# Seventeen unread transposes of the identity at the start, and two tiles' second halves put one place later, in an encoder layer's kernel

## The chip, the cores and the metric

One core of a Trainium2 chip runs the whole program; the other cores are idle. The metric is the device time of one execution in microseconds (us), and less is better. TensorE (PE) does the matrix products, VectorE (DVE) and ScalarE (ACT) the elementwise work, GpSimd (POOL) and SyncE (SP) mostly issue DMAs.

## What is computed

One encoder layer on 1024 tokens of width 1024, in float32: a half-step feed-forward block, two groups of attention heads side by side, and a second half-step feed-forward block. The change touches only the first microseconds of the first block:

```python
def rmsnorm(x, g):
    xf = x.astype(jnp.float32)
    y = xf * lax.rsqrt(jnp.mean(xf * xf, axis=-1, keepdims=True) + NORM_EPS)
    return (y * g.astype(jnp.float32)).astype(x.dtype)

def swiglu(x, w_gate, w_up, w_down):
    return (jax.nn.silu(x @ w_gate) * (x @ w_up)) @ w_down
...
        h = swiglu(rmsnorm(x, ffn1_pre_g[l]), ffn1_w_gate[l], ffn1_w_up[l], ffn1_w_down[l])
        x = x + 0.5 * rmsnorm(h, ffn1_post_g[l])
...
```

## The kernel before, in words

**Tiles.** The 1024 tokens are eight tiles of 128 rows. A tile `t` is loaded, normalised (`xn`), and turned on TensorE in two halves of 512 columns: four transposes of 128x128 fill one PSUM bank (`trp`, pool `pst`, two banks). ScalarE rounds the bank to a high part, VectorE subtracts to get the low part. The first halves of tiles 0 to 3 make up operand `A11` (`x_161` high, `x_162` low), the second halves `A12` (`x_163`, `x_164`). `Operand.one(t)` turns the next half of tile `t`; with a list `later` it puts off the copy and the store (`keep`) of that half.

**Products.** Every product is three TensorE passes, high by high (L354), high by low (L355), low by high (L356), and is called for four slices of 128 rows (`ks`), so one block of 512 columns is 12 matmuls. The gate weights come in column blocks b = 0, 1, 2, ...: `graw` is loaded by SP (L480), ACT casts it to `whi` (L453), DVE subtracts to `wlo` (L454), in `split_left`. Blocks 0 to 2 are handled by hand in `begin`; from block 3 on `PairGemm.ahead` does them. In its order TensorE computes block 0 with A12, block 1 with A12, block 3 with A11, block 2 with A12, block 4 with A11, block 3 with A12, and so on. After a block's A12 product VectorE adds the kept A11 result (L657, tile `s`, in place) and ScalarE applies SiLU (L659), whose first use loads a table. The A11 result was copied from PSUM by `save` (L472) and stored to memory (`s1d<-s`).

**Order.** Inside `begin` a manual schedule fixes the order of TensorE, VectorE and ScalarE as the code is written. `begin` ends by giving VectorE and ScalarE back to the scheduler; only TensorE stays in written order. From there on the scheduler places the casts, subtractions, SiLUs and squares of `ahead`, by its own estimate of when each is ready. `c.step()` runs inside `PairGemm.mm` after every second slice: it takes one step off the list `c.steps`, so that a half-tile's transposes can be put in the middle of a product.

**Start.** The gain row is spread over 128 partitions by two float32 matmuls with one row of ones (L341, `gps`). Before them TensorE has nothing to do, and after them it waits for the first normalised tile. Then it turns the first halves of tiles 0 and 1, multiplies blocks 0 and 1 by their 256 columns, turns the first halves of tiles 2 and 3, and finishes. In the last loop of `begin`, over the three blocks, the second halves of tiles 0 to 3 are turned.

Of the kernel before, what the change touches and what calls it, by code (L numbers as in the profile page):

```python
# [10 lines left out]
F32 = mybir.dt.float32  # L11
# [8 lines left out]
P, T = 128, 512  # L20
# [148 lines left out]
def transposed(c, x, bank=False):  # L169

    ps = (c.psm.tile([P, 4, P], F32, tag="mm", name="trp") if bank else
          c.pst.tile([P, 4, P], F32, tag="tr", name="trp"))
    for j in range(4):
        c.nc.tensor.transpose(ps[:, j, :], x[:, j * P:(j + 1) * P], c.ident)  # L174
    return ps


def transpose_in(c, x, hi, lo):

    ps = transposed(c, x)  # L180
    c.nc.scalar.copy(hi, ps)
    c.nc.vector.tensor_sub(lo, ps, hi.bitcast(F32))  # L182
    return ps


class Operand:
# [59 lines left out]
    def one(self, t, later=None):  # L246
# [6 lines left out]
        if t < 4:  # L253
            if t not in self.raw:
                two = c.xp.tile([P, 2, 2, 4, P], F32, tag="s", name="raw", bufs=c.deep)
                self.raw[t], self.raw[t + 1] = two[:, 0], two[:, 1]
            raw, i = self.raw[t], 0 if b == A11 else 1
            hi, lo = [h[:, :, cols] for h in self.x[b]]

            def keep():  # L260
                c.nc.scalar.copy(raw[:, i], ps)
                c.nc.gpsimd.dma_start(self.saved[t][:, i], raw[:, i].rearrange("p k x -> p (k x)"))
            if later is None:
                ps = transposed(c, src)
                c.nc.scalar.copy(hi, ps)
                keep()
                c.nc.vector.tensor_sub(lo, raw[:, i], hi.bitcast(F32))
            else:
                ps = transpose_in(c, src, hi, lo)
                later.append(keep)  # L270
        elif b == A11:
            while self.open == c.deep:
                c.sums.popleft()()
            self.open += 1
            self.left_half(t, src)
        else:
            self.right_half(t, src, cols)

    def left_half(self, t, src):

        c = self.c
        s = c.xp.tile([P, 4, 4, P], F32, tag="s", name="s", bufs=c.deep)
        c.nc.scalar.copy(s[:, 0], transposed(c, src, t > 4))
        self.half[t] = s, self.half[t]
# [49 lines left out]
def spread_gain(c, t, row, one):  # L334

    nc = c.nc
    copies = []
    for h in range(2):
        sl = slice(h * T, h * T + T)
        ps = c.psm.tile([P, T], F32, tag="mm", name="gps")  # L340
        nc.tensor.matmul(ps, one, row[:, sl], start=True, stop=True)  # L341
        copies.append(lambda sl=sl, ps=ps: nc.scalar.copy(t[:, sl], ps))
    return t, *copies
# [998 lines left out]
def layer(tc, a, out):  # L1342
    nc = tc.nc
    c = Ctx(tc)
    with ExitStack() as ctx:
# [81 lines left out]
        def ffn(which, op, prep, pg, get, turns, sums, more, post, pre, src, dst, begin=None, tables=()):  # L1427
# [7 lines left out]
            if begin:  # L1435
                left_pool(e)
            begun = begin(pg) if begin else ()
            plan(pg.early, turns)
            r = sub()
# [119 lines left out]
        with ExitStack() as order:  # L1559
# [16 lines left out]
            op0 = Operand(c, None, 0)  # L1576
            nc.gpsimd.memset(xn[1][:1, :P], 1.0)
            for t in range(2):
                for h, q in enumerate((nc.sync, nc.scalar)):
                    q.dma_start(xs[t][:, half[h]], x0[t][:, half[h]])  # L1580
                    if (t, h) == (0, 0):
                        nc.sync.dma_start(xn[0][:1], a["ffn1_pre_g"])
            op0.gain, *gains = spread_gain(c, gain, xn[0][:1], xn[1][:1, :P])

            def begin(pg):
                for b in range(2):
# [62 lines left out]
                keeps = []  # L1649
# [26 lines left out]
                scaled(r1, 1, 2, 3)  # L1676
                hi2(1)
                for b in range(3):
                    if b == 1:
                        c.steps.extend(lambda t=t: op0.one(t) for t in range(2))  # L1680
                    elif b:
                        op0.one(2, keeps)
                        c.steps.append(lambda: op0.one(3, keeps))
                    pg.mm(acc[b], pg.w[b], 0, A11, cols=slice(256 if b < 2 else 0, 512))
                    s1.append(pg.save(b, acc[b]))
                    (lo0, lo1, lo2)[b](1)
                while keeps:
# [8 lines left out]
                                    {0: [F(4, 5), L(6, 7)], 2: [F(6, 7)], 3: [U(4)], 5: [U(5)], 6: [U(6)], 7: [U(7)]},  # L1696
                                    down_sums(a["wd1"], ts1), value_sums(a["wv"], tsv),
                                    a["ffn1_post_g"], a["mix_pre_g"], x0, x1, begin,
                                    bias_steps(c, *[a[k] for k in ("na_rel_bias", "t5_rel_bias", "onehot", "lncount", "cmask")]))

# [293 lines left out]
```

## Time and profile before

| | us |
|---|---|
| median of 3 runs | 1843.02 (1842.95 to 1844.0) |
| the profiled execution, its own time | 1842.29 |
| its span, first to last instruction | 1840.3 |
| TensorE busy | 1817.0 (99%) |
| VectorE busy | 1329.6 (72%) |
| ScalarE busy | 829.9 (45%) |
| GpSimd busy | 322.4 (18%) |

The span is 1.99 us shorter than the execution's own time, and that execution is 0.73 us below the median of the three runs. Times in the views are counted from the first instruction. In a timeline a row gives start, duration, engine, line, operation, output and inputs, and in brackets the idle time before it with what ended it; matmuls overlap, so their pace is read from start to start. In a view by windows each row gives the stretch, then the busy time of each engine with the number of instructions, the clock granted to TensorE, the share of the DMA engines and their rate.

### The profile page before, as it was taken

How to read it: one execution, taken by the hardware profiler on the slowest of the kernel's cores; microseconds unless marked ns; L12 is line 12 of the kernel's file. 1: busy time of each engine (PE TensorE's matmuls, PEld its weight loads, DVE VectorE, ACT ScalarE, POOL GpSimd, SP SyncE). 2: the span in 40 equal slices, each digit the busy share in tenths (PEclk: the TensorE clock that was granted, in tenths of full speed). 3: DMA queues.
4: the chain of work that ended last, by engine and by line, in shares of the span. 5: the costliest groups of instructions: out<-in, count | busy, mean ns of one | idle time of the engine just before them, and what ended most of it. 6: DMA issues, size and time to landing. Idle time of an engine off the chain costs nothing.

```text
span 1840.3 us, 25143 instructions
## 1 busy us (share of the span) xinstructions
PE 1817.0 (99%) x8904; PEld 1527.5 (83%) x8904; DVE 1329.6 (72%) x2243; ACT 829.9 (45%) x1479; POOL 322.4 (18%) x508
## 2 busy tenths in 40 slices
PE   7999999999999999999999999999999999999998
PEld 6887888888888888888899998878888888888886
DVE  5878877776566877477777866778888777754557
ACT  6622233334443657133688765564222333354433
POOL 2223211111121122132333100121111111110000
PEclk9999999999999999999999999999999999999999
DMA  7756565657888857869686532595556566596564
GB/s 274 240 176 226 170 227 208 222 184 252 315 295 314 285 198 260 275 209 305 201 276 217 183 125 94 184 311 183 178 169 212 191 218 233 183 343 204 186 226 150
DMA packets 172991, 409.66 MB, mean 223 GB/s; under 512 B 20081, under 2 KB 42513, under 8 KB 170818
## 3 DMA queue, kind: packets, MB, share of 16 engines
q1 hardware_dynamic: 124706, 246.33, 40.6%
q0 software_dynamic: 47152, 159.64, 23.7%
q10 hardware_dynamic: 1008, 2.10, 0.3%
q8 instruction: 70, 1.15, 0.3%
q14 instruction: 55, 0.45, 0.1%
HBM read 280.49 MB, written 132.56 MB: 224 GB/s over the span
## 4 chain that ended last, share of the span: by engine, by line
PE 89%; DVE 4%; ACT 2%; issue 2%; DMA 2%; POOL 0%; SPq 0%; DVEq 0%; POOLq 0%; ACTq 0%
PE mmp L356 17%; PE mmp L354 17%; PE mmp L355 17%; PE accp L354 10%; PE accp L356 10%; PE accp L355 10%; PE po L1161 2%; PE po L1274 2%; PE ptp L1057 2%; PE trp L174 1%; PE sp L1258 1%; PE sp L1140 1%; DVE pw L738 1%; ACT pb L1049 1%; DMA s1d<-s 0%
## 5 line engine op out<-in xcount | busy, mean ns | idle before, releaser
L354 PE MATMUL mmp<-x,whi 128*128 128x512 f32 (+1 forms) x1464 | 572.7, 391 | 1.7 <-ACT whi L453 1.1
L356 PE MATMUL mmp<-x,wlo 128*128 128x512 f32 (+1 forms) x1464 | 570.2, 389 | 3.8 <-DVE wlo L454 3.8
L355 PE MATMUL mmp<-x,whi 128*128 128x512 f32 (+1 forms) x1464 | 570.1, 389 | 0.5 <-DVE x L182 0.3
L356 PEld LDWEIGHTS mmp<-x,wlo 128*128 128x128 f32 x1464 | 276.2, 189 | 62.2 <-DVE wlo L454 5.5
L354 PEld LDWEIGHTS mmp<-x,whi 128*128 128x128 f32 x1464 | 276.1, 189 | 59.9 <-issue 1.7
L355 PEld LDWEIGHTS mmp<-x,whi 128*128 128x128 f32 x1464 | 276.2, 189 | 56.9 <-DVE x L182 1.2
L738 DVE TENSOR_TENSOR pw<-praw,pw 128x1024 fp32r<-128x1024 f32 (+1 forms) x181 | 200.4, 1151 | 122.4 <-ACT pw L737 121.9
L737 ACT CAST pw<-praw 128x1024 fp32r<-128x1024 f32 (+1 forms) x181 | 168.4, 981 | 204.7 <-PE accp L356 167.7
L354 PE MATMUL accp<-pw 128*128 128x512 f32 x600 | 234.4, 391 | 0.0
L356 PE MATMUL accp<-pw 128*128 128x512 f32 x600 | 233.6, 389 | 0.0
L355 PE MATMUL accp<-pw 128*128 128x512 f32 x600 | 233.5, 389 | 0.0
L453 ACT CAST whi<-wraw 128x1024 fp32r<-128x1024 f32 x126 | 132.4, 1053 | 221.3 <-PE mmp L355 182.9
L454 DVE TENSOR_TENSOR wlo<-wraw,whi 128x1024 fp32r<-128x1024 f32 x126 | 154.6, 1229 | 20.5 <-ACT whi L453 19.2
L356 PEld LDWEIGHTS accp<-pw 128*128 128x128 f32 x600 | 112.6, 188 | 23.5
L355 PEld LDWEIGHTS accp<-pw 128*128 128x128 f32 x600 | 112.7, 188 | 23.2
L354 PEld LDWEIGHTS accp<-pw 128*128 128x128 f32 x600 | 112.7, 188 | 23.2 <-ACT hb L781 0.2
L453 ACT CAST whi<-traw 128x512 fp32r<-128x512 f32 x52 | 32.3, 622 | 157.6 <-DVE traw L545 104.4
L680 POOL DMA_DIRECT2D g<-sg x44 | 23.9, 543 | 428.6 <-DVE sg L673 239.9
L632 DVE TENSOR_TENSOR c<-mmp,u 128x512 f32<-128x512 f32 x52 | 35.9, 691 | 72.8 <-PE mmp L356 72.7
L472 ACT COPY s<-mmp 128x512 f32<-128x512 f32 x52 | 30.6, 588 | 121.3 <-PE mmp L356 113.9
L544 DVE TENSOR_TENSOR wraw<-wraw 128x1024 f32<-128x1024 f32 x52 | 63.6, 1223 | 13.1 <-DMA wraw<-in_wu_dram 12.2
L619 DVE TENSOR_TENSOR c<-mmp,v 128x512 f32<-128x512 f32 x52 | 35.7, 686 | 32.5 <-PE mmp L356 32.5
(286 smaller groups left out, 2775.4 us busy)
## 6 DMA issues: line engine op xcount, KB each, us to landing
praw<-g SPq DMA_DIRECT2D x70, 512.0 KB, 5.7
wraw<-in_wg_dram SPq DMA_DIRECT2D x44, 512.0 KB, 4.2
wraw<-in_wu_dram SPq DMA_DIRECT2D x44, 512.0 KB, 6.8
tr<-in_wd_dram SPq DMA_DIRECT2D x44, 512.0 KB, 6.6
g<-sg POOLq DMA_DIRECT2D x88, 256.0 KB, 5.0
ts<-tr POOLq DMA_DIRECT2D x22, 1024.0 KB, 4.7
praw<-ts SPq DMA_DIRECT2D x88, 256.0 KB, 3.8
praw<-in_wd_dram SPq DMA_DIRECT2D x66, 256.0 KB, 5.6
```

Of the source, the lines that this page charges most:

```text
L354: nc.tensor.matmul(out, ahi, bhi, start=start, stop=False, skip_group_check=go_on)
L355: nc.tensor.matmul(out, ahi, blo, start=False, stop=False, skip_group_check=go_on)
L356: nc.tensor.matmul(out, alo, bhi, start=False, stop=stop, skip_group_check=go_on)
L453: nc.scalar.copy(hi, raw)
L454: nc.vector.tensor_sub(lo, raw, hi.bitcast(F32))
L544: nc.vector.tensor_sub(r[:, 0:2], r[:, 1:3], r[:, 0:2])
L632: c.behind(lambda: nc.vector.tensor_add(c21, d, u2), *((DVE,) if self.sink.soon and b == self.n - 1 else ()))
L737: nc.scalar.copy(hi, raw[:, :m])
L738: nc.vector.tensor_sub(lo, raw[:, :m], hi.bitcast(F32))
L1057: nc.tensor.transpose(ps[:, j, :], src[:, j * P:(j + 1) * P], c.ident)
L1161: nc.tensor.matmul(po[:, un * 2 + j], pt[:, 2 * j + t, :], rhs, start=t == 0, stop=t == 1)
L1274: nc.tensor.matmul(po[0][:, u], pt[0][:, j, :], vs[:, k0 + j, :], start=j == 0, stop=j == n - 1)
```

## The change

A new helper `turned(c, n)` takes a `trp`-sized bank and turns the identity into it n times; nothing reads the bank. It is called with 13 ahead of the two gain matmuls and with 4 behind them. In the last loop of `begin` the second halves of tiles 2 and 3 are both queued as steps inside block 2's product; before, tile 2 was turned ahead of that product, and tile 3 was its first step.

```diff
+def turned(c, n):
+
+    ps = c.pst.tile([P, 4, P], F32, tag="tr", name="turned")
+    for j in range(n):
+        c.nc.tensor.transpose(ps[:, j % 4, :], c.ident, c.ident)
...
+            turned(c, 13)
             op0.gain, *gains = spread_gain(c, gain, xn[0][:1], xn[1][:1, :P])
+            turned(c, 4)
...
                 for b in range(3):
-                    if b == 1:
-                        c.steps.extend(lambda t=t: op0.one(t) for t in range(2))
-                    elif b:
-                        op0.one(2, keeps)
-                        c.steps.append(lambda: op0.one(3, keeps))
+                    if b:
+                        c.steps.extend(lambda t=t: op0.one(t, *([keeps] if t > 1 else [])) for t in (2 * b - 2, 2 * b - 1))
                     pg.mm(acc[b], pg.w[b], 0, A11, cols=slice(256 if b < 2 else 0, 512))
```

Seven lines come ahead of everything that is named here, so L354 of before is L361 of after, L453 is L460, and so on.

TensorE in block 2's product, before (`trp<-ident,x` turns a half of tile 2 or 3, `x_161` is A11, `x_163` is A12; the first row turns tile 1):

```order
L174 MATMUL trp<-ident,xn 128x128 x4
L174 MATMUL trp<-ident,x 128x128 x4
L354 MATMUL mmp<-x_161,whi 128x512
L355 MATMUL mmp<-x_162,whi 128x512
L356 MATMUL mmp<-x_161,wlo 128x512
L354 MATMUL mmp<-x_161,whi 128x512
L355 MATMUL mmp<-x_162,whi 128x512
L356 MATMUL mmp<-x_161,wlo 128x512
L174 MATMUL trp<-ident,x 128x128 x4
```

Six more matmuls of A11 follow there, then block 0's A12 product. The same engine after, from the middle of block 2's product to the first A12 matmuls:

```order
L174 MATMUL trp<-ident,x 128x128 x4
L361 MATMUL mmp<-x_161,whi 128x512
L362 MATMUL mmp<-x_162,whi 128x512
L363 MATMUL mmp<-x_161,wlo 128x512
L361 MATMUL mmp<-x_161,whi 128x512
L362 MATMUL mmp<-x_162,whi 128x512
L363 MATMUL mmp<-x_161,wlo 128x512
L174 MATMUL trp<-ident,x 128x128 x4
L361 MATMUL mmp<-x_163,whi 128x512
L362 MATMUL mmp<-x_164,whi 128x512
```

Each of the two sets of transposes has moved six matmuls later, and tile 3's now stands right in front of the product that reads it.

ScalarE behind `begin`, before (`x2` squares tiles 4 and 5; `whi<-graw` are the weight blocks 3, then 4; `s_362` and `s_399` are the results of blocks 0 and 1):

```order
L166 ACTIVATE xn,ss<-x 128x1024 x2
L659 ACT_TABLE_LOAD
L659 ACTIVATE s_362<-s_362 128x512
L453 CAST whi<-graw 128x1024
L659 ACTIVATE s_399<-s_399 128x512
L166 ACTIVATE xn,ss<-x 128x1024
L453 CAST whi<-graw 128x1024
```

And after (the same two results are `s_381` and `s_418`):

```order
L166 ACTIVATE xn,ss<-x 128x1024 x2
L460 CAST whi<-graw 128x1024
L666 ACT_TABLE_LOAD
L666 ACTIVATE s_381<-s_381 128x512
L460 CAST whi<-graw 128x1024
L666 ACTIVATE s_418<-s_418 128x512
L166 ACTIVATE xn,ss<-x 128x1024
```

The scheduler has moved the cast of block 3 ahead of the table load and the first SiLU, and the cast of block 4 ahead of the second SiLU and a square.

VectorE at the same place, before (`wlo<-graw,whi` is block 3; `s_399` is the sum for block 1; the small rows are the scale factors of tiles 4 and 5, the L226 row their normalisation):

```order
L151 TENSOR_SCALAR y<-y 128x2
L157 TENSOR_TENSOR e<-y,v 128x2
L158 TENSOR_TENSOR e<-e,y 128x2
L159 SCALAR_TENSOR_TENSOR y<-e,y 128x2
L157 TENSOR_TENSOR e<-y,v 128x2
L158 TENSOR_TENSOR e<-e,y 128x2
L159 SCALAR_TENSOR_TENSOR y<-e,y 128x2
L157 TENSOR_TENSOR e<-y,v 128x2
L158 TENSOR_TENSOR e<-e,y 128x2
L657 TENSOR_TENSOR s_399<-mmp,s_399 128x512
L159 SCALAR_TENSOR_TENSOR y<-e,y 128x2
L226 SCALAR_TENSOR_TENSOR xn<-x,y,gain 128x1024
```

The row behind these is L454, the subtraction for block 3. After, from the same row on:

```order
L151 TENSOR_SCALAR y<-y 128x2
L461 TENSOR_TENSOR wlo<-graw,whi 128x1024
L157 TENSOR_TENSOR e<-y,v 128x2
L158 TENSOR_TENSOR e<-e,y 128x2
L159 SCALAR_TENSOR_TENSOR y<-e,y 128x2
L664 TENSOR_TENSOR s_418<-mmp,s_418 128x512
```

The subtraction for block 3 has moved ahead of the sum for block 1 and of a normalisation. Apart from the places named here, the order of the instructions on each engine is the same in both programs, save that the subtraction for block 4 and the pieces of the scale factors also change places next to these rows.

## The prediction

> **What bounds the kernel now.** I read the page first, then the busy time in 40 windows.
>
> ```profile
> span 1840.3 us, 25143 instructions
> PE 1817.0 (99%) x8904; PEld 1527.5 (83%) x8904; DVE 1329.6 (72%) x2243; ACT 829.9 (45%) x1479; POOL 322.4 (18%) x508
> ```
> ```profile
> 46.00:92.00 46.00, 46.00 (x218) 38.09 (x217) 37.97 (x63) 30.02 (x49) 9.61 (x18) 1.00 0.70 240
> ```
>
> TensorE sets the time: of 1840.3 us it is idle for 23.3, and from 46 us on it is full. All that the change moves lies ahead of 46 us. Behind it every load is issued as a buffer is given back, that is, relative to the work, so I count a microsecond won or lost ahead of 46 us as one microsecond of the end.
>
> The timeline ahead of 46 us has one large hole, at block 3's product with A11:
>
> ```profile
> 34.02 0.50 PE L354 MATMUL mmp<-x,whi 128*128 128x512 f32 x1 [1.06 <-ACT whi L453]
> 34.35 0.40 PE L355 MATMUL mmp<-x,whi 128*128 128x512 f32 x1
> 37.31 0.50 PE L356 MATMUL mmp<-x,wlo 128*128 128x512 f32 x1 [2.56 <-DVE wlo L454]
> 40.85 0.63 PE L354 MATMUL mmp<-x,whi 128*128 128x512 f32 x1
> ```
>
> TensorE idles 1.06 us for block 3's `whi`, does two matmuls, idles 2.56 us for its `wlo`, and begins block 2's product with A12 only at 40.85. The rows of ScalarE and VectorE say why both parts are late:
>
> ```profile
> 30.88 0.21 ACT L166 ACTIVATION_READ_ACCUMULATOR xn<-x 128x1 f32 x1
> 31.11 1.28 ACT L659 ACT_TABLE_LOAD   x1
> 32.94 1.03 ACT L453 CAST whi<-graw 128x1024 fp32r<-128x1024 f32 x1
> ...
> 31.53 0.17 DVE L151 TENSOR_SCALAR y<-y 128x2 int32<-128x2 int32 x1
> 34.04 0.69 DVE L657 TENSOR_TENSOR s<-mmp,s 128x512 f32<-128x512 f32 x1 [0.77 <-DMA s1d<-s]
> 36.03 1.22 DVE L454 TENSOR_TENSOR wlo<-graw,whi 128x1024 fp32r<-128x1024 f32 x1
> ```
>
> The cast stands behind the table load and the first SiLU. The subtraction stands behind block 1's sum, which waits until 34.04 for a store of the tile that it overwrites, and then behind a normalisation. Neither waits for the weights: block 3 is asked for at 23.50 and takes 8.0 us, so it is there at 31.5.
>
> ```profile
> 23.50 16.44 SPq L480 DMA_DIRECT2D graw<-in_wg_dram  x4
> ...
> graw<-in_wg_dram SPq DMA_DIRECT2D x1, 512.0 KB, 8.0
> ```
>
> The hole has a second price. I cut the start into stretches of 3.41 us (columns: stretch, length, TensorE busy, then the others; the granted clock is third from the end):
>
> ```profile
> 4.27:7.68 3.41, 3.06 (x4) 1.16 (x4) 1.08 (x5) 2.50 (x6) 0.00 (x0) 1.00 0.99 364
> 7.68:11.09 3.41, 2.40 (x9) 1.57 (x8) 2.61 (x7) 2.74 (x5) 0.00 (x0) 1.00 1.02 377
> 11.09:14.51 3.42, 2.60 (x11) 2.08 (x10) 3.05 (x9) 2.46 (x8) 0.00 (x0) 1.00 0.32 129
> 14.51:17.92 3.41, 3.41 (x18) 3.41 (x17) 1.83 (x5) 2.30 (x5) 1.24 (x2) 1.00 0.11 44
> 34.98:38.40 3.42, 1.09 (x5) 0.92 (x6) 3.42 (x4) 2.50 (x4) 0.55 (x1) 1.00 1.00 375
> 38.40:41.81 3.41, 3.41 (x10) 2.65 (x9) 1.19 (x2) 0.59 (x1) 0.00 (x0) 0.50 1.03 416
> ```
>
> In 34.98 to 38.40 TensorE was busy for 1.09 us, and for the next 3.41 us its clock is 0.50; then it is full again. Half of that stretch, 1.7 us, is lost. It is part of the 40.85 above.
>
> **The change, part by part.**
>
> *The seventeen transposes* run where TensorE has nothing to do.
>
> ```profile
> 1.12 0.28 POOL masks.py:199 TENSOR_SCALAR_AFFINE_SELECT ident<-ident 128x128 f32<-128x128 f32 x1
> 4.62 3.75 PE L341 MATMUL gps<-xn 1*128 1x512 f32 x4 [4.62 <-DMA xn<-in_ffn_pre_g_dram]
> 9.38 1.94 PE L174 MATMUL trp<-ident,xn 128*128 128x128 f32 x8 [1.01 <-DVE xn L1615]
> 11.36 0.58 ACT L181 CAST x<-trp 128x512 fp32r<-128x512 f32 x1 [0.27 <-PE trp L174]
> 13.10 0.42 PE L356 MATMUL mmp<-x,wlo 128*128 128x256 f32 x1
> 13.31 0.41 PE L354 MATMUL mmp<-x,whi 128*128 128x256 f32 x1
> 15.44 1.06 ACT L261 COPY raw<-trp 128x512 f32<-128x512 f32 x2
> 16.51 1.72 PE L174 MATMUL trp<-ident,x 128*128 128x128 f32 x8
> 17.61 1.25 ACT L181 CAST x<-trp 128x512 fp32r<-128x512 f32 x2 [1.11 <-PE trp L174]
> 17.99 0.36 PE L354 MATMUL mmp<-x,whi 128*128 128x256 f32 x1
> ```
>
> The eight transposes from 16.51 to 17.99 take 0.185 us each, those at 9.38 at most 1.94 / 8 = 0.24. Thirteen are 2.4 to 3.1 us, from the finished identity at 1.40 to 3.8 or 4.5: ahead of the gain row that lands at 4.62. Four are 0.74 to 0.97 us, from 8.37 to 9.1 or 9.34: ahead of the normalised tile at 9.38. Their cost is 0, at most 0.1 us, and nobody waits for their bank.
>
> What they may win is the clock. At 13.10 a matmul of 256 columns starts every 0.21 us; later one of 512 columns starts every 0.23 (27.01 to 27.25 to 27.47, rows below). So TensorE runs at half pace to 17.9 or so, though the clock column shows 1.00 there; six stretches of 3.41 us ahead of 38.40 is 17.92, and the stretch that ends there was the first to be wholly busy, 3.41 of 3.41. Busy shares of 2.40, 2.60 and even 3.06 us (the gain matmuls, one row high) did not do. With the fillers a stretch of 3.41 us that begins at 0.85 holds 13 x 0.185 = 2.4 us, the next is 4.27 to 7.68 as before, and 7.68 to 11.09 gains 0.74 and holds 3.1. None is full if the stretches fall as in this execution. If they fall with a start between 4.62 and 5.7, one lies wholly inside the gain matmuls and the four transposes behind them, which is a third of the places that it can have, and that helps only if those one-row matmuls count. I take 0 for the clock, with 1.1 to 1.4 us as the other end: if it is full ahead of 13.10, the matmuls from there to 16.51 take half, tiles 2 and 3 are turned as soon as they are scaled, and their casts begin when ScalarE is free, at 15.44 + 1.06 = 16.50 and not at 17.61: 1.1 us, and 0.27 more from the earlier cast at 11.36.
>
> The Trainium skill, in TensorE: Matmul & The Clock Gate, Part 1, says that the gate watches a free-running window of 3413 ns and opens after one busy window; the two edges of the 0.50 stretch here agree. Its Part 4 says of transposes on TensorE that "it doesn't count as PE-busy the same way", which would make these seventeen worth nothing and give the same sum as mine. The trace speaks against that: of the full stretch 14.51 to 17.92, 1.41 us were transposes (from 16.51 on) and 2.0 us matmuls, and the stretch ahead of it, busy for 2.60 us with nearly nothing but matmuls, had not brought the full clock.
>
> *Tiles 2 and 3 later.* The rows of before:
>
> ```profile
> 23.54 0.66 PE L174 MATMUL trp<-ident,x 128*128 128x128 f32 x4
> 25.42 0.60 PE L174 MATMUL trp<-ident,x 128*128 128x128 f32 x4
> 26.05 0.59 ACT L181 CAST x<-trp 128x512 fp32r<-128x512 f32 x1 [0.44 <-PE trp L174]
> 26.67 0.69 DVE L182 TENSOR_TENSOR x<-trp,x 128x512 fp32r<-128x512 f32 x1
> 27.01 0.39 PE L356 MATMUL mmp<-x,wlo 128*128 128x512 f32 x1
> 27.25 0.39 PE L354 MATMUL mmp<-x,whi 128*128 128x512 f32 x1
> 27.47 0.45 PE L355 MATMUL mmp<-x,whi 128*128 128x512 f32 x1
> ```
>
> Tile 3's transposes at 25.42 are cast from 26.05 (0.63 later) and subtracted from 26.67 to 27.36, under six matmuls; the A12 product then needs the low part at 27.47, and it is there. After the change that cover is gone. Block 2's product starts some 0.27 us before 23.54, since it needn't wait for a free bank, so tile 3's transposes start at 23.27 + six matmuls 1.47 + transposes 0.35 + six matmuls 1.48 = 26.6; cast at 27.2, subtraction 27.8 to 28.5, and the second A12 matmul at 28.5 instead of 27.47. Cost 1.1 us. From below: with the transposes' own latency hidden, 0.6. The same moved step takes the stores of the two halves and the save of block 2's result 0.4 us later in POOL's queue and on ScalarE; nobody waits for these here.
>
> *The new order behind it.* Both casts and the subtraction of block 3 now stand ahead of what made them late. From 28.5 on there are 11 matmuls left of block 0 with A12, then 12 of block 1: at 0.23 us each, block 3's product is wanted at 28.5 + 23 x 0.23 = 33.8, and its third matmul, the first that needs `wlo`, at 34.3. ScalarE is through with the second square at 31.1, with the 0.4 us from above 31.5, and the weights are there at 31.5: cast to 32.5. VectorE has done L151 by then (31.7 plus at most 0.8 of the later sum for block 0), subtraction to 33.8. Both are ready, by 1.3 and 0.5 us. So no hole, and no half clock after it: block 3's twelve matmuls end at 33.8 + 12 x 0.23 = 36.6, where block 2 with A12 begins. Before that was 40.85. Gain 4.25 us, with the 1.1 us lost at tile 3 already in it.
>
> *Sum.* Fillers 0, tile 3 and the new order together -4.25: 1842.29 - 4.25 = 1838.0 by the profiled execution. That one lies 0.73 below the median of the three runs, so the same sum against the median is 1838.8.
>
> **The rivals.**
>
> 1. *The clock opens early as well.* For it: the transposes count, by the stretch to 17.92. Against it: no stretch was full in the phase of this execution. All behind 16.5 us, loads too, moves up by 1.1 to 1.4: 1836.6 to 1836.9.
> 2. *The hole comes back in part, from the memory.* The cast now stands first and would hold ScalarE until its weights land. In the same stretch a load of the same size took 9.5 us:
>
> ```profile
> x<-in_x_dram POOLq DMA_DIRECT2D x1, 512.0 KB, 9.5
> ...
> sgd<-s POOLq DMA_DIRECT2D x1, 256.0 KB, 6.9
> ```
>
> Then the weights are there at 33.0, the cast ends at 34.0 and the subtraction at 35.3, 1.0 us after TensorE wants it: 1839.0. With a short idle stretch that halves the clock again for up to 3.41 us, another 1.7: 1840.7.
> 3. *Slower: a new wait on ScalarE.* Block 0's SiLU is now behind the cast, at 33.8 to 34.5, and its store starts then. Block 3's save needs that store's buffer; at 6.9 us the store is through at 41.4, and ScalarE, in order, holds block 5's cast behind it: save 0.6, cast 1.03, subtraction 1.22, ready at 44.3. TensorE wants it after three products of 2.76 and two sets of transposes, at 36.6 + 9.0 = 45.6. It is hidden by 1.3 us. It decides when the store takes over 8.2 us, and makes the kernel slower than before by 0.2% when it takes 8.2 + 4.25 + 3.7 = 16.1 us, which no row comes near.
> 4. *That the change doesn't do what it says*: the fillers leave the clock as it is. That is my forecast.
>
> **How the numbers follow.** Forecast 0.50; early clock 0.27; part of the hole back 0.18; slower 0.05. The executions of before differ by 1.7 us, which I put down to where the stretches fall. The range 1836.0 to 1840.2 takes in the early clock below and most of the second rival above. A measurement of this kernel can tell about 0.2%, 3.7 us, from no change: the line is 1839.3. The forecast is under it by 1.3, and I give it 0.46 of its 0.50 there; the early clock all of its 0.27; the second rival 0.03 of 0.18. Faster 0.76, same 0.19, slower 0.05.
>
> **What would show it.** Right: block 3's first three matmuls in a row near 33.8 with no wait on `whi` or `wlo`; no stretch of clock 0.50 at 38; a new wait of about 1 us in front of the first A12 matmuls, on the cast and the subtraction of tile 3. The early clock shows in matmuls of 256 columns every 0.12 us at 13. Wrong: a wait of block 3 on its cast with the cast waiting for the load, or block 5 waiting for its cast.

## The result, and the profile after

The changed kernel takes 1838.11 us, the median of 9 runs (1836.71 to 1841.1), against 1843.01 for the kernel before (9 runs beside them, 1840.68 to 1844.82). The ratio is 0.9973, with a 95% interval of 0.9964 to 0.9982: 3.3 to 6.6 us faster. The forecast was 1838.0 in a range of 1836.0 to 1840.2. The profiled execution's own time is 1838.41.

The page of the changed kernel, and its first 46 us as one window (columns as in the prediction); the same window of before stands behind it:

```profile
span 1836.4 us, 25177 instructions
PE 1819.0 (99%) x8921; PEld 1529.0 (83%) x8921; DVE 1328.5 (72%) x2243; ACT 829.6 (45%) x1479; POOL 324.7 (18%) x508
0.00:46.00 46.00, 41.84 (x194) 33.19 (x195) 28.25 (x60) 30.95 (x56) 12.82 (x31) 1.00 0.74 276
```
```profile
0.00:46.00 46.00, 35.56 (x155) 27.63 (x156) 27.26 (x58) 29.72 (x53) 11.98 (x30) 0.96 0.74 274
```

TensorE's idle time ahead of 46 us has shrunk from 10.44 to 4.16 us. That is no measure of the gain, since 3.04 + 1.12 us of the new busy time are the transposes that nobody reads (that this sum is 4.16 as well is chance):

```profile
1.46 3.04 PE L182 MATMUL turned<-ident 128*128 128x128 f32 x13 [1.46 <-POOL ss L1643]
8.13 1.12 PE L182 MATMUL turned<-ident 128*128 128x128 f32 x4
```

The gain is read from where the work stands. The hole at block 3 is gone; TensorE's timeline after:

```profile
25.86 0.60 PE L174 MATMUL trp<-ident,x 128*128 128x128 f32 x4
27.14 0.50 PE L361 MATMUL mmp<-x,whi 128*128 128x512 f32 x1 [0.68 <-ACT x L188]
27.86 0.50 PE L362 MATMUL mmp<-x,whi 128*128 128x512 f32 x1 [0.22 <-DVE x L189]
...
33.19 0.39 PE L361 MATMUL mmp<-x,whi 128*128 128x512 f32 x1
...
33.64 0.39 PE L363 MATMUL mmp<-x,wlo 128*128 128x512 f32 x1
...
35.91 0.39 PE L361 MATMUL mmp<-x,whi 128*128 128x512 f32 x1
...
38.63 0.39 PE L361 MATMUL mmp<-x,whi 128*128 128x512 f32 x1
```

Tile 3's high and low part are waited for, as forecast; block 3's first three matmuls follow each other every 0.23 us; block 2 with A12 begins at 35.91 and not at 40.85. The engines that feed it, ScalarE and VectorE:

```profile
16.96 1.07 ACT L188 CAST x<-trp 128x512 fp32r<-128x512 f32 x2 [0.65 <-PE trp L174]
...
30.80 1.05 ACT L460 CAST whi<-graw 128x1024 fp32r<-128x1024 f32 x1 [0.17 <-DMA graw<-in_wg_dram]
...
31.88 1.23 DVE L461 TENSOR_TENSOR wlo<-graw,whi 128x1024 fp32r<-128x1024 f32 x1
```

Tiles 2 and 3 are cast from 16.96 (17.61 before). Block 3's cast runs at 30.80 where it ran at 32.94, the subtraction at 31.88 where it ran at 36.03. There is no half clock left. Before, the clock was 0.50 from 38.40 to 41.81; after, it is 1.00 there:

```profile
38.00:40.00 2.00, 2.00 (x11) 1.60 (x10) 1.46 (x2) 0.00 (x0) 0.00 (x0) 1.00 1.03 412
40.00:42.00 2.00, 2.00 (x13) 1.70 (x12) 0.00 (x0) 0.00 (x0) 0.00 (x0) 1.00 1.02 416
```

And there is a new wait, which the prediction had priced at nothing:

```profile
34.09 0.55 POOL L670 DMA_DIRECT2D sgd<-s  x1 [2.39 <-ACT s L666]
...
41.83 0.60 PE L174 MATMUL trp<-ident,xn 128*128 128x128 f32 x4
...
42.31 0.59 ACT L479 COPY s<-mmp 128x512 f32<-128x512 f32 x1 [6.01 <-DMA sgd<-s]
42.95 0.50 PE L361 MATMUL mmp<-x,whi 128*128 128x512 f32 x1 [0.52 <-ACT s L479]
```

Block 3's save takes over the buffer of block 0's SiLU. That tile's store is asked for at 34.09 and the save starts at 42.31. TensorE waits 0.52 us, because from block 3 on the A12 product goes on in the very PSUM bank that the save copies (VectorE adds a kept A11 result for blocks 0 to 2 only). In the kernel before, the same matmul follows its transposes without a wait:

```profile
44.03 0.39 PE L354 MATMUL mmp<-x,whi 128*128 128x512 f32 x1
...
47.23 0.60 PE L174 MATMUL trp<-ident,xn 128*128 128x128 f32 x4
47.58 0.48 PE L354 MATMUL mmp<-x,whi 128*128 128x512 f32 x1
```

From those transposes to that matmul it is 0.35 us before and 1.12 after, so the wait costs 0.77 us from start to start.

### The profile page after: what moved, and what is told of

It reads as the page before. It is cut to its first block, busy times and chain, and to the rows that moved or that the text cites. A ratio compares the mean times of both kernels' runs of the same rounds, so it can differ in the third digit from the quotient of the medians.

```text
span 1836.4 us, 25177 instructions
## 1 busy us (share of the span) xinstructions
PE 1819.0 (99%) x8921; PEld 1529.0 (83%) x8921; DVE 1328.5 (72%) x2243; ACT 829.6 (45%) x1479; POOL 324.7 (18%) x508
## 4 chain that ended last, share of the span: by engine, by line
PE 76%; issue 11%; DVE 5%; DMA 3%; ACT 2%; POOL 1%; DVEq 0%; POOLq 0%; SPq 0%; ACTq 0%
PE mmp L363 13%; PE mmp L361 13%; PE mmp L362 13%; PE accp L363 9%; PE accp L362 9%; PE accp L361 9%; PE po L1168 2%; PE po L1281 2%; PE ptp L1064 2%; PE sp L1265 1%; PE trp L174 1%; PE sp L1147 1%; DVE pw L745 1%; POOL g L711 1%; ACT pb L1056 1%
## 5 line engine op out<-in xcount | busy, mean ns | idle before, releaser
L361 PE MATMUL mmp<-x,whi 128*128 128x512 f32 (+1 forms) x1464 | 571.9, 391 | 1.9 <-ACT x L188 1.4
L361 PEld LDWEIGHTS mmp<-x,whi 128*128 128x128 f32 x1464 | 275.7, 188 | 59.8 <-ACT x L188 2.2
L361 PE MATMUL accp<-pw 128*128 128x512 f32 x600 | 234.3, 391 | 0.2 <-ACT hb L788 0.2
L460 ACT CAST whi<-wraw 128x1024 fp32r<-128x1024 f32 x126 | 132.6, 1054 | 221.3 <-PE mmp L362 182.8
L361 PEld LDWEIGHTS accp<-pw 128*128 128x128 f32 x600 | 112.6, 188 | 23.8 <-ACT hb L788 0.6
L460 ACT CAST whi<-traw 128x512 fp32r<-128x512 f32 x52 | 32.3, 621 | 157.4 <-DVE traw L552 110.3
```

Of the source, the lines that this page charges most:

```text
L361: nc.tensor.matmul(out, ahi, bhi, start=start, stop=False, skip_group_check=go_on)
L460: nc.scalar.copy(hi, raw)
```

## The experiments

Theory 1 was the prediction's: the whole gain is the scheduler's new order of block 3's cast and subtraction, and the transposes do nothing. Theory A was that the transposes open the clock early and this carries part of the gain. The first four kernels tell these apart; the other seven ask why an earlier start isn't worth more. All but `fill40` were timed in five rounds beside the kernel before (medians 1843.07, 1842.96 and 1842.95 in the three sets).

### The transposes alone

Against the changed kernel, the tiles go back to their place of before:

```diff
-                    if b:
-                        c.steps.extend(lambda t=t: op0.one(t, *([keeps] if t > 1 else [])) for t in (2 * b - 2, 2 * b - 1))
+                    if b == 1:
+                        c.steps.extend(lambda t=t: op0.one(t) for t in range(2))
+                    elif b:
+                        op0.one(2, keeps)
+                        c.steps.append(lambda: op0.one(3, keeps))
```

> Only the seventeen transposes are added; tiles 2 and 3 stay in the order of before, and with them the order of ScalarE and VectorE. Theory 1 (the whole gain comes from the order of the casts, which the moved tiles changed): about 1843, within 1 us of before, with the hole at block 3 from 34 to 37 us and the half clock after it still there. Theory 2 (the fillers open the clock early): matmuls of 256 columns start every 0.12 us at 13, and 1841.6 to 1842.

1843.02 us (11 runs), ratio 0.9999 (0.999 to 1.0008). The scheduler's orders on ScalarE and VectorE are those of before. TensorE's timeline, and a window behind the hole:

```profile
33.30 0.50 PE L361 MATMUL mmp<-x,whi 128*128 128x512 f32 x1 [1.08 <-ACT whi L460]
...
37.29 0.79 PE L363 MATMUL mmp<-x,wlo 128*128 128x512 f32 x1 [3.26 <-DVE wlo L461]
...
38.00:40.00 2.00, 2.00 (x6) 1.53 (x5) 1.56 (x2) 0.00 (x0) 0.00 (x0) 0.50 1.02 412
```

The hole and the half clock are both there. The seventeen transposes show no gain by themselves. The interval reaches from 1.8 us faster to 1.5 slower, so the 1.1 to 1.4 us of an early clock are not excluded by this time alone; in the profiled execution the matmuls of 256 columns kept their half pace up to 15.8.

### The moved tiles alone

Against the changed kernel, the transposes are left out:

```diff
-            turned(c, 13)
...
-            turned(c, 4)
```

> Only tiles 2 and 3 are moved, no fillers; ScalarE and VectorE have the order of the changed kernel. Theory 1: as the changed kernel, 1838.1, within 1 us. Theory 2 (the fillers carry 1.1 to 1.4 us of the gain): 1839.2 to 1839.5.

1838.47 us (11 runs), ratio 0.9977 (0.9968 to 0.9986): as much as the changed kernel gains, within the intervals. Tile 3's lost cover is there, the hole is not:

```profile
27.93 0.50 PE L361 MATMUL mmp<-x,whi 128*128 128x512 f32 x1 [0.68 <-ACT x L188]
...
36.72 0.39 PE L361 MATMUL mmp<-x,whi 128*128 128x512 f32 x1
```

### The new order without the move

The tiles stay where they were and no transposes are added; block 3's cast and subtraction are written ahead of block 0's sum and SiLU, so that the scheduler places them first. Against the kernel before:

```diff
                 self.mm(a, w, 1, A12, s1 is None)
+                if b == 0 and begun:
+                    self.split_left(3)
```

> The tiles stand as in before and there are no fillers, but block 3's cast and subtraction are written ahead of block 0's SiLU, so that ScalarE and VectorE get nearly the changed kernel's order. Theory 1 (the order of the casts is all of it, and the moved tiles cost TensorE 0.6 to 1.1 us): no hole at block 3, A12 of block 0 starts 0.6 to 1.1 us earlier than with the moved tiles. If nothing is late behind that, 1837.0 to 1837.5. If the save of block 3, which waits for the store of block 0's SiLU, decides the start of block 3's A12 product, it comes at the same time as before it, TensorE waits there about 1.7 us instead of 0.8, and the time is 1838.1. Theory 2 (the place of the transposes itself matters): 1843.

1838.69 us (8 runs), ratio 0.9974 (0.9964 to 0.9985). The move of the tiles is one way to the new order and not the only one. The tile's 1.1 us that this version saves are not seen in the time. In its profiled execution the first tile is turned at 11.52 (9.38 before), and block 3 waits for its weights:

```profile
34.13 1.05 ACT L453 CAST whi<-graw 128x1024 fp32r<-128x1024 f32 x1 [0.98 <-DMA graw<-in_wg_dram]
...
35.23 0.50 PE L354 MATMUL mmp<-x,whi 128*128 128x512 f32 x1 [0.25 <-ACT whi L453]
...
36.49 0.50 PE L356 MATMUL mmp<-x,wlo 128*128 128x512 f32 x1 [0.52 <-DVE wlo L454]
```

That is the prediction's second rival, at 0.77 us.

### Forty transposes

```diff
-            turned(c, 13)
+            turned(c, 40)
```

> The changed kernel with 40 transposes ahead of the gain matmuls instead of 13: at 0.22 us each at half clock they last 8.8 us from 1.5, so a stretch of 3.41 us of nothing but transposes fits wherever the stretches fall. Theory A (transposes open the clock): by 8.3 us the pace of the transposes doubles, the gain matmuls take 0.43 us each and not 0.86, the 256-column matmuls start every 0.12 us from the first. The start is delayed by 0 to 2 us, and the time is 1837 to 1840. Theory B (they do not count): the pace stays 0.21 us up to the first stretch full of matmuls, the first tile is turned some 4 us later, and the time is 1841 to 1843.

One run, 1839.86 us. TensorE's timeline:

```profile
1.46 7.03 PE L182 MATMUL turned<-ident 128*128 128x128 f32 x40 [1.46 <-POOL ss L1643]
8.42 1.98 PE L348 MATMUL gps<-xn 1*128 1x512 f32 x4
...
15.09 0.28 PE L361 MATMUL mmp<-x,whi 128*128 128x256 f32 x1
15.20 0.28 PE L362 MATMUL mmp<-x,whi 128*128 128x256 f32 x1
```

The gain matmuls take 1.98 us instead of 3.75, and matmuls of 256 columns start every 0.12 us instead of 0.21. Transposes do open the clock. By Part 4 of TensorE: Matmul & The Clock Gate, in the Trainium skill, they would not; this run decides against it. The price here is that the gain matmuls start at 8.42, 4.0 us later than in the changed kernel.

### The changed kernel again

> The changed kernel once more, beside the next three on the same chip: 1838 within 1 us, the wait of block 3's A12 product for its save 0 to 0.8 us.

1837.9 us (9 runs), ratio 0.9975 (0.9965 to 0.9984). Its profile began later (first tile turned at 10.59 and not 9.17), and the first A12 matmul of block 3 follows its transposes after 0.45 us, 0.10 more than before, not 0.77. So the size of the new wait differs from execution to execution.

### An earlier table load

A SiLU of one column inside `begin` loads ScalarE's table there, so that the table load no longer stands between block 3's cast and block 0's SiLU.

```diff
+                nc.scalar.activation(c.small.tile([P, 4], F32, tag="e", name="e")[:, :1], c.ident[:, :1], AF.Silu)
```

> The changed kernel with one SiLU of a single column on ScalarE at about 16.3 us, where it waits for TensorE, so that the table of SiLU is loaded there and not in front of block 0's SiLU. Theory 1 (block 3's save waits for the store of block 0's SiLU, and TensorE for the save): the SiLU, its store and the save come up to 1.28 us earlier, the 0.77 us that TensorE waits there are gone, and the time is 1837.3 to 1837.9, at worst 0.3 us are lost on the casts at 17. Theory 2 (that wait is covered again later): as the changed kernel.

1838.74 us (11 runs), ratio 0.998 (0.9971 to 0.9989): no gain. The table load now stands ahead of the casts of tiles 2 and 3, which begin at 17.97, for 16.96 in the changed kernel's profile; a part of that is the clock, which opened only near 18.5 here. Block 0's SiLU follows block 3's cast at once, at 33.04, and the save still waits for the store:

```profile
16.57 1.28 ACT L1672 ACT_TABLE_LOAD   x1
...
17.97 1.13 ACT L188 CAST x<-trp 128x512 fp32r<-128x512 f32 x2
...
32.08 1.05 ACT L460 CAST whi<-graw 128x1024 fp32r<-128x1024 f32 x1 [0.46 <-DMA graw<-in_wg_dram]
...
42.75 0.59 ACT L479 COPY s<-mmp 128x512 f32<-128x512 f32 x1 [5.58 <-DMA sgd<-s]
```

### The store in another queue

The stores of the first three SiLUs are issued by ScalarE, not by GpSimd.

```diff
-            nc.gpsimd.dma_start(d, sg)
+            (nc.scalar if s1 is not None else nc.gpsimd).dma_start(d, sg)
```

> The changed kernel, with the stores of the SiLU of blocks 0 to 2 issued by ScalarE's own DMA queue instead of GpSimd's. In the changed kernel the store of block 0's SiLU is asked for at 34.09 and block 3's save waits for it until 42.31, a wait that costs TensorE 0.77 us. Theory 1 (the store is late because it stands in GpSimd's queue behind the loads and stores of the tiles): on a queue of its own it lands by 40, the save stands right behind the last A11 matmul of block 3, the wait is gone, and the time is 1837.1 to 1837.5. Theory 2 (all transfers share one throughput, the queue is indifferent): it lands at 42 or later, the wait stays at 0.8 us or grows, and the time is 1838.0 to 1838.6.

1838.16 us (9 runs), ratio 0.9977 (0.9967 to 0.9986). The time is the one that this run's theory 2 forecast. The DMA issue of the store, what follows it, the stores by their group, and a window:

```profile
35.87 0.33 ACTq L670 DMA_DIRECT2D sgd<-s  x1
...
44.28 0.59 ACT L479 COPY s<-mmp 128x512 f32<-128x512 f32 x1 [5.42 <-PE trp L174]
...
sgd<-s ACTq DMA_DIRECT2D x2, 256.0 KB, 8.3
...
40.00:44.00 4.00, 4.00 (x23) 3.31 (x21) 1.42 (x2) 0.00 (x0) 0.00 (x0) 1.00 1.02 407
```

In a queue of its own the 256 KB take 8.3 us, no less than in GpSimd's. The DMA share is 1.02 there, which fits transfers that wait for each other whatever queue they are in; what they wait for is not shown. The releaser named for the save, a transpose, is put down to the wrong one: the four transposes at 43.67 write another bank, while 35.87 + 8.3 = 44.2, with the median of the two stores in that window, is about the store's landing. TensorE waits 0.66 us for the save.

### Three ways to an early clock

`rows128`: twenty transposes, and gain matmuls of 128 rows, 127 of them zero.

```diff
-            nc.gpsimd.memset(xn[1][:1, :P], 1.0)
+            nc.gpsimd.memset(xn[1][:, :P], 1.0)
+            nc.vector.memset(xn[0], 0.0)
...
-            turned(c, 13)
-            op0.gain, *gains = spread_gain(c, gain, xn[0][:1], xn[1][:1, :P])
+            turned(c, 20)
+            op0.gain, *gains = spread_gain(c, gain, xn[0], xn[1][:, :P])
```

> The changed kernel with 20 transposes ahead of the gain matmuls instead of 13, and with the gain matmuls 128 rows high instead of one: 127 rows of zeros below the gain row, ones under all of them, the same result. TensorE is then busy without a gap from 1.5 to about 9.3 us, as it nearly is in the changed kernel. Theory A (matmuls of one row do not count for the clock, transposes and full matmuls do): the clock opens by 8.3 us wherever the stretches fall, 256-column matmuls start every 0.12 us from the first, everything behind 16.5 moves up by 1.1 to 1.4, 1836.7 to 1837.0. Theory B (it is not the rows; the gain matmuls or the mix of both don't count): pace 0.21 up to 16 us or later, 1838.1, or up to 0.3 more if the gain row comes later.

1838.29 us (11 runs), ratio 0.9977 (0.9968 to 0.9986). The gain matmuls ran at full pace (1.96 us), but at 13.81 matmuls of 256 columns started every 0.21 us again: the clock had opened and closed. The save cost more here: block 3's first A12 matmul waited 0.85 us for it.

`best` adds to this the early table load and the early cast of block 3, on the tiles' order of before.

> All that should help together: tiles 2 and 3 as before the change, block 3's cast written ahead of block 0's SiLU, the table of SiLU loaded early, 20 transposes and gain matmuls of 128 rows. If the early clock gives 1.1 to 1.4, the covered casts of tile 3 0.6 to 1.1 and the earlier save lets them through: 1835.6 to 1836.4. If the weights of block 3, which come from memory, set its start: no better than the better of the two before it, 1836.7 to 1837.3, with a wait of block 3's cast for its load.

1840.45 us (11 runs), ratio 0.9988 (0.9979 to 0.9997): slower than the changed kernel and than either time that was expected. In its profile block 2 with A12 begins at 36.75 and then TensorE waits longest of all for the save:

```profile
43.90 0.59 ACT L479 COPY s<-mmp 128x512 f32<-128x512 f32 x1 [6.72 <-DMA sgd<-s]
44.54 0.50 PE L361 MATMUL mmp<-x,whi 128*128 128x512 f32 x1 [1.29 <-ACT s L479]
```

Another part lies in the early table load. It runs from 16.57 to 17.85, as in the version that has it alone, and the casts of tiles 2 and 3 stand behind it at 17.97. Here the clock had been open since 16.0 and the tiles were turned from 16.31, so TensorE waited 0.99 us for these casts; in `rows128`, with the casts at 17.25, it didn't wait. The two waits are what the rows show, in an execution whose own time is 1839.87; whether they make up the whole of some 2.3 us stays open.

`held` is `rows128` with 14 transposes behind the gain matmuls and ten more ahead of the first product, to keep the clock open; `held_act` adds the stores in ScalarE's queue.

```diff
-            turned(c, 4)
+            turned(c, 14)
...
+                for j in range(10):
+                    nc.tensor.transpose(acc[2][:, j % 4 * P:j % 4 * P + P], c.ident, c.ident)
```

> The changed kernel with 20 transposes of the identity ahead of the gain matmuls, those matmuls 128 rows high, 14 transposes behind them and ten more between the first tiles' transposes and the first product, so that an early opened clock has less idle time in which to close. Both theories expect matmuls of 256 columns every 0.12 us near 13. Theory 1 (a microsecond won at the start is one of the end): block 0's product with A12 begins 1.1 to 1.4 us earlier and the time is 1836.7 to 1837.1. Theory 2 (the memory paces blocks 3 to 5): what is won is waited for again in front of block 3's cast and its save, whose wait of 0.8 us grows to 1.5 to 2.2, and the time is 1837.6 to 1838.6.

> Both edits together: the clock kept open by transposes, and the SiLU stores of blocks 0 to 2 in ScalarE's queue. If the store's queue is what makes block 3's save wait, both gains stand: 1835.8 to 1836.5. If the memory's throughput paces the stage whatever the queue, the time is that of the other two within 0.6 us, 1837.6 to 1838.6.

1838.68 us (10 runs, ratio 0.9973, 0.9964 to 0.9983) and 1838.34 us (9 runs, 0.9975, 0.9965 to 0.9984). In the profiled execution of `held` the gain matmuls still ran at half pace (3.66 us) and the first tile was turned at 12.07, 2.9 us later than in the changed kernel; the clock opened as they ended, since the 14 transposes behind them took 1.69 us, as long as the same 14 in `held_act`. In that of `held_act` it was open before the first tile and stayed so. What became of it is seen in TensorE's and ScalarE's rows:

```profile
10.29 1.38 PE L174 MATMUL trp<-ident,xn 128*128 128x128 f32 x8
...
13.41 0.28 PE L361 MATMUL mmp<-x,whi 128*128 128x256 f32 x1
13.53 0.28 PE L362 MATMUL mmp<-x,whi 128*128 128x256 f32 x1
...
16.42 1.26 PE L174 MATMUL trp<-ident,x 128*128 128x128 f32 x8 [0.94 <-ACT raw L268]
...
15.79 1.06 ACT L268 COPY raw<-trp 128x512 f32<-128x512 f32 x2
17.11 1.19 ACT L188 CAST x<-trp 128x512 fp32r<-128x512 f32 x2 [0.26 <-PE trp L174]
```

TensorE is done with its matmuls at 15.48 and waits until 16.42 for a bank: the copies of tiles 0 and 1 out of the two `trp` banks run from 15.79 to 16.85 on ScalarE. Tiles 2 and 3 are cast from 17.11; in the changed kernel, at half pace, they were cast from 16.96. But the first tile was turned at 10.29 here and at 9.17 there. From it to these casts it is 6.82 us in `held_act`, and 6.6 to 6.8 in the other three profiles with the clock open at the first tile and no early table load (in `rows128` it was shut again in between), against 7.79 in the changed kernel and 8.23 (9.38 to 17.61) before. So the open clock does shorten this path, by 1.0 to 1.4 us, until the copies on ScalarE end it; the later first tile takes that back. How much of the lateness the added work causes isn't separated: the changed kernel's second profile has its first tile at 10.59.

## Why the prediction was right, point by point

**The bound.** It took a microsecond ahead of 46 us as one of the end. That can now be tested over many starts. From block 3's first A12 matmul to the end of the span:

| | block 3 with A12 | span | rest |
|---|---|---|---|
| before | 47.58 | 1840.3 | 1792.7 |
| transposes alone | 48.72 | 1841.5 | 1792.8 |
| after | 42.95 | 1836.4 | 1793.5 |
| after, again | 43.71 | 1837.4 | 1793.7 |
| tiles alone | 43.01 | 1836.3 | 1793.3 |
| earlier table load | 43.39 | 1835.8 | 1792.4 |
| `held_act` | 42.85 | 1836.3 | 1793.5 |
| store in ScalarE's queue | 44.92 | 1838.3 | 1793.4 |

The rest is 1792.4 to 1793.7 for starts that lie 5.9 us apart: one for one, to within 0.7 us either way. The five executions that aren't listed give 1792.6 to 1793.8. The changed kernel's execution gives back 0.7 of its 4.63 there, 0.5 of it by 500 us and 0.2 near 1230. That is inside the scatter, and what it consists of wasn't tried.

**The transposes: cost 0, gain 0.** Right as far as the times tell. Alone they give a ratio of 0.9999, and the tiles alone give the changed kernel's time. The first rival, the early clock, didn't come about: in the changed kernel's profile the pace changed at 16.33. Its size was sound: where the clock was open at the first tile, the path to the casts of tiles 2 and 3 was 1.4 us shorter than before, for 1.1 to 1.4 forecast. Those versions turn their first tile 1.1 to 2.9 us later than the changed kernel's first profile, so their times don't show it. The rival's step "tiles 2 and 3 are turned as soon as they are scaled" also fell short, since they need the banks that ScalarE's copies hold; that put the casts 0.26 behind the copies.

**Tile 3's lost cover: 1.1 us.** Right. The second A12 matmul came at 27.86 for 27.47 before, 0.39 late; at the last transposes of tile 1, at 22.20 for 22.92, the execution was 0.72 early, so 1.11 us were lost between.

**The hole, -4.25 with that loss.** Right, and somewhat more: 35.91 - 40.85 = -4.94. The 0.7 more came ahead of it: tile 3's transposes stand at 25.86, where the prediction had 26.6. This execution's clock opened at 16.3 and not at 17.9, and tiles 2 and 3 were cast 0.65 us earlier. With the tiles alone the same matmul starts at 36.72, 0.1 from the forecast of 36.6. That the transposes opened the clock sooner here isn't shown: with the same seventeen the pace changed near 15.9 in the version without the moved tiles and near 18.5 in that with the earlier table load. One term was also left out: the half clock of before ran on to 41.81, so block 2's product with A12 took 3.18 us (40.85 to 44.03) and now takes 2.72 (35.91 to 38.63). These 0.46 us the prediction had taken for a part of the 40.85.

**The second rival, the memory.** It holds in part. The cast now waits for the weights, 0.17 us here and 0.98 in the version with the early cast, where TensorE lost 0.77.

**The third rival, the save: "hidden by 1.3 us".** Here a step failed. The prediction held the save's wait against block 5's cast only, at 45.6. It overlooked that block 3's A12 product writes the bank that the save reads, so the save is wanted right behind the transposes that start at 41.83. It was also short on the store: 6.9 us taken, 8.2 measured, with a DMA share of 1.02 to 1.03 in the windows shown. The price from start to start was 0.77 us in this profile, 0.10 in the second one of the same kernel, 0.02 in that of the tiles alone, and 1.54 at most, in `best`. This cost and the 0.46 us of gain that were left out partly cancel, which is luck.

**The sum.** The two profiled executions differ by 1842.29 - 1838.41 = 3.88 us, the medians by 4.90; the forecast of 4.25 lies between. In the profiled execution the hole gave 0.7 more than reckoned and the end of the half clock 0.46, the save took 0.77 back, and 0.7 went in small steps behind 46 us: 4.25 + 0.69 + 0.46 - 0.77 - 0.73 = 3.90, the difference of the spans. That the median came within 0.1 us of 1838.0 is closer than the working deserves: the same sum taken from the median of before is 1838.8, as the prediction says itself, and executions of one kernel lie up to 4.4 us apart (1836.71 to 1841.1).

## What to carry to other kernels

Where code is placed by a scheduler, compare its order before and after ahead of costing an edit: here a step moved one place later cost 1.1 us where it stands, and won some 5 us because a cast and a subtraction changed places with work that waited. When a stall of several microseconds goes, look at every reader and writer of the buffers behind it, PSUM banks included, for who now comes late; and ask what the memory allows. In this stage the DMA share was about 1, and another queue for the store gained nothing; a version that moves fewer bytes there was not tried.

## What the runs showed of the hardware

The clock can open on transposes and shut again before it is used. In the profiled execution with the stores in ScalarE's queue:

```profile
1.45 3.03 PE L182 MATMUL turned<-ident 128*128 128x128 f32 x13 [1.45 <-POOL ss L1643]
4.42 2.20 PE L348 MATMUL gps<-xn 1*128 1x512 f32 x4
6.54 0.66 PE L182 MATMUL turned<-ident 128*128 128x128 f32 x4
10.58 1.97 PE L174 MATMUL trp<-ident,xn 128*128 128x128 f32 x8 [3.38 <-DVE xn L1624]
```

The four gain matmuls took 2.20 us, not 3.75, and four transposes 0.66; behind 3.38 us of idleness the next eight took 1.97 again, half pace. With the same thirteen transposes the changed kernel's profiled execution kept half pace until 16.33, though TensorE's records leave no gap from 1.46 to 9.25:

```profile
2.68:6.09 3.41, 3.41 (x11) 2.24 (x10) 0.54 (x1) 2.10 (x4) 0.00 (x0) 1.00 0.96 357
6.09:9.50 3.41, 3.41 (x9) 1.38 (x8) 2.28 (x10) 2.46 (x7) 0.00 (x0) 1.00 1.00 372
12.92:16.33 3.41, 3.41 (x18) 3.41 (x17) 3.07 (x11) 2.72 (x6) 0.20 (x1) 1.00 0.00 0
```

These are stretches of 3.41 us counted back from 16.33, where the pace changed. The first two were wholly busy, largely with gain matmuls one row high, and did not open the clock; the last did. (In the one left out, 9.50 to 12.92, TensorE had idle time.) That one-row matmuls count for less fits this, and fits `held`, where 3.66 us of gain matmuls 128 rows high were followed by the open clock. No run isolates it: in `rows128` the clock was open before they began.
